# An MLA gate product with x stationary and 512 weight columns moving, and block copies from DRAM to DRAM during attention

## The chip, the cores and the metric

The kernel runs on one core of a Trainium2 chip. Its time is the time of one execution on the device, in microseconds (us); lower is better. Three runs of the kernel before gave 1257.67 to 1261.07 us, with a median of 1259.69 us. Profiles come from one further execution, recorded by the hardware profiler.

The engines are TensorE (PE; its weight loads are PEld), VectorE (DVE), ScalarE (ACT), GpSimd (POOL) and SyncE (SP). TensorE multiplies a stationary 128x128 operand by a moving operand of up to 512 columns into PSUM. SP does no arithmetic here: it issues nearly all DMAs, one after the other, and waits in its queue for what each of them needs.

## What is computed

One layer of a hybrid encoder, on x of 2048 tokens by 1024. One input projection feeds two mixers: GLA (gated linear attention, 4 heads of 128) and MLA (latent attention, 4 heads of 128). Each mixer's output is gated, both are laid side by side, projected, added to x, and normalized:

```python
h = x @ w_in
g_q, g_k, g_v, g_gate, g_lr_f, g_lr_b, m_cq, m_ckv, m_kr, m_gate = split(h)
o_a = rms_norm(o_fwd + o_bwd, norm_g) * silu(g_gate)     # GLA
o_b = softmax(scores(m_cq, m_ckv, m_kr)) @ v * silu(m_gate)   # MLA
x = layer_norm(ALPHA * x + concat([o_a, o_b]) @ w_out)
```

The change is about `silu(m_gate)`, with `m_gate = x @ w` of 2048 x 512, and about how it and `o_a` get from tokens on partitions to channels on partitions, as the last projection needs them. Every product is made in float32 with each operand split into a high and a low part (`hi` rounds, `lo` subtracts) and three matmuls: high by high, high by low, low by high (`mm3`, L417).

## The kernel before

**Stages.** Sweep A (from the start to about 345 us of the span) goes over 16 chunks of 128 tokens and makes GLA's intra-chunk part and gate. Sweep C (about 345 to 580) goes over 8 steps of two chunks. Attention (about 580 to 1110) goes over 16 blocks, each of one head and 512 queries, and over 8 pairs of key tiles in a block; towards its end the output projection begins, whose 16 chunks run until the end.

**Sweep C, one step.** For each chunk: `ipm` (L1341, the projection to cq, ckv and kr), `Ob` (L1506, GLA's inter-chunk part), then `oib`, `sqO`, `ss`, `rgl`, `rgd`, `og` (the norm and gate of GLA's output, L1509 to L1530), `oT` (a transpose in blocks of 32x32 on VectorE) and `soT` (its store to `oa_s`). From the same `ipm` come `sqm`, `ssm`, `rml`, `rmd`, `cq` (the norm of cq), then `tm` (L1413, TensorE transposes), `cqTh`, `cqTl`, `pqr` (L1437, the rotary query), `qrf` to `qrTl`, and once a step `pq` (L1296, the absorbed query) with `qah`, `qal` and `sqa` (its high and low part and their stores).

**The gate product before.** `pz` (L1257 to L1273) is made once a step, with 128 weight columns stationary and x of both chunks moving, 256 columns: 4 heads x 8 slices of the model dimension x 3 = 96 matmuls in 8 parts of 12. The result has channels on partitions already. `gm1`, `gm2`, `gm3` (ACT: exp, ln, exp on 1024 columns) and `gm4` (DVE) make the silu, `sgm` stores it to `gm_s`, whose rows here are 256 columns.

**The order of the work.** Tables written by hand set it: `PLACE_C`, with `PLACE_C_FIRST` and `PLACE_C_LAST` for the first and last step (L147 to L344). Each operation has a place in units of steps, of the step it belongs to; two values are those of the two chunks, eight those of the parts of `pz`. `sweep_c` sorts all by step plus place, and each engine, SP too, runs its own in exactly that order (`in_order`, L381). So an instruction that waits holds back all that its engine has behind it. Attention has such tables as well (`PLACE`, `PLACE_LAST`, `PLACE_OUT`), with a key-tile pair as the unit and 8 units to a block.

**Buffers.** PSUM tiles of tag "gp" (two buffers) hold `pz`, `Ob` and `pq` in turn. In SBUF, tag "gm" has one buffer, which serves the gate's `gm` and then `qal` of the same step; tag "og" has two, for `og`. A tile that takes over a buffer waits for the last user of it, which for a stored tile is the landing of its store.

**Attention's DMAs.** `fetch` (L1567), ten DMAs on SP a block, brings the queries of the block after next; `yc` (L1773) stores a block's output to `ob_s`.

**The output projection.** `OutProj.load` (L1944) issues seven DMAs on SP for a chunk: four of `oa_s` to `of`, each putting 32x32 blocks in place by rows of 32 numbers (128 bytes; `blocks_of`, L1142), one each of `gm_s` and of the softmax sums `r_s` to `gr`, and one of `ob_s` to `of`. `gate` (L1962, POOL) multiplies, `hi` (ACT) and `lo` (POOL) split, `part` and `product` (L1988, L1996) make the matmuls (`po`, `pmb`, `px`), `residual` and `finish` (L2026, L2035) add x and normalize on VectorE, and SP stores the rows.

Of the kernel before, what the change touches and what calls it, by code (L numbers as in the profile page):

```python
# [23 lines left out]
H = 4  # L24
# [108 lines left out]


SETUP_C = ("lset", "u15", "u14", "wS", "wH", "wL", "pb0", "wa0", "wh0", "wl0", "pb1", "wa1", "wh1", "wl1")
STEP_C = ("gm1", "gm2", "gm3", "gm4", "sgm", "pq", "qah", "qal", "sqa")
CHUNK_C = ("lx", "xh", "xl", "lS", "lq", "lo", "lu", "sqm", "ssm", "rml", "rmd", "cq", "ckv", "krf", "krfa",
    "krsh", "krsl", "vh", "vl", "kvx", "tm", "cqTh", "cqTl", "ckvTh", "ckvTl", "krT", "pqr", "qrf", "qrfa",
    "tq", "qrTh", "qrTl", "Sf1", "Sf2", "M", "Ob", "oib", "sqO",
    "ss", "rgl", "rgd", "og", "oT", "soT")  # L140

FETCH_C = ("lx", "xh", "xl")
LAST_C = ("ckvTh", "ckvTl", "krT")
# [51 lines left out]
    lx=(-0.578, -0.186),  # L195
    soT=(1.119, 1.45),
    pz=(0.25, 0.306, 0.318, 0.429, 0.527, 0.531, 0.557, 0.559),
    gm1=0.823,
    gm2=0.832,
    gm3=0.837,  # L200
    gm4=0.845,
    sgm=1.17,
    pq=1.435,
    qah=1.501,
# [69 lines left out]
    gm1=0.643,  # L274
    gm2=0.815,
    gm3=0.82,
    gm4=0.83,
    sgm=1.056,
    pq=1.431,
    qah=1.57,  # L280
# [8 lines left out]
    ipd=(0.042, 0.445),  # L289
    Ob=(0.0, 0.425),  # L290
    tm=(0.495, 1.083),
    pqr=(0.749, 1.284),
    tq=(0.95, 2.1),
    xh=(-0.262, -0.109),
    sqO=(0.15, 0.435),
# [18 lines left out]
    krf=(0.139, 0.6),  # L314
    cqTl=(0.598, 1.211),
    ckvTl=(0.88, 1.703),
    qrf=(0.795, 1.556),
    qrTl=(1.081, 2.186),
    xl=(-0.244, 0.3),
    M=(-0.531, -0.11),  # L320
# [2 lines left out]
    krfa=(0.255, 0.636),  # L323
    krsl=(0.395, 0.879),
    vl=(0.968, 2.242),
    qrfa=(0.871, 2.029),
    lS=(-0.721, -0.203),
    lq=(-0.357, 0.05),
    lo=(-0.14, 0.045),
# [1 line left out]
    lx=(-0.48, -0.573),  # L331
    soT=(1.29, 2.304),
    pz=(0.572, 0.578, 0.707, 0.845, 0.918, 1.023, 1.1, 1.22),
    gm1=1.309,
    gm2=1.608,
    gm3=1.859,
    gm4=1.953,
    sgm=2.042,
    pq=1.525,
    qah=1.948,  # L340
# [13 lines left out]
class K:  # L354
# [151 lines left out]
    def run(self):  # L506
        tc, nc, ins = self.tc, self.nc, self.ins
        with ExitStack() as top:
            cp = top.enter_context(tc.tile_pool(name="const", bufs=1))
            self.cp = cp  # L510
            dp = top.enter_context(tc.tile_pool(name="scr", bufs=1, space=DRAM))
            self.qd_s = [dp.tile([P, H * P], F32, name=f"qd_s{c}") for c in range(NCH)]
            self.oi_s = [dp.tile([P, H * P], F32, name=f"oi_s{c}") for c in range(NCH)]
            self.su_s = [dp.tile([P, H * P], F32, name=f"su_s{c}") for c in range(NCH)]
            self.u_s = [dp.tile([P, H * P], F32, name=f"u_s{c}") for c in range(NCH)]
            self.qa_s = [[dp.tile([P, H, QB], F32, name=f"q{p}_s{b}") for p in "hl"] for b in range(NQB)]
            self.qr_s = [dp.tile([2, QB // P, P, 256], F32, name=f"qr_s{b}") for b in range(NQB)]
# [737 lines left out]


    def c_pz(self, s, n):  # L1257
        last = s["st"] == NCH // 2 - 1
        if n == 0:
            s["pz"] = self.gp.tile([P, H, 256], F32, tag="gp", name=f"pz{s['st']}")  # L1260
        order = [(h, k) for h in range(H) for k in range(NK)]
        if last:
            order = [(h, k) for p in range(2) for k in range(NK) for h in (p, p + 2)]
        x2 = lambda t, k: t[:, k].rearrange("p a t -> p (a t)")
        part = [(h, k, p) for h, k in order[4 * n:4 * n + 4] for p in range(3)]
        if n == 0 and s["st"]:

            part.sort(key=lambda e: e[2] == 1)
        stop = {h: (k, p) for h, k, p in part if k == NK - 1}
        for h, k, p in part:  # L1270
            w, x = ((0, self.xch), (0, self.xcl), (1, self.xch))[p]
            self.nc.tensor.matmul(s["pz"][:, h], self.Wz[k][w][:, h * P:(h + 1) * P], x2(x, k),  # L1272
                                  start=(k == 0 and p == 0), stop=stop.get(h) == (k, p))  # L1273

    def c_gm1(self, s):
        s["gm"] = self.w1.tile([P, H, 256], F32, tag="gm", name=f"gm{s['st']}")
        self.nc.scalar.activation(s["gm"], s["pz"], AF.Exp, scale=-1.0)

    def c_gm2(self, s):
        self.nc.scalar.activation(s["gm"], s["gm"], AF.Ln, bias=1.0)  # L1280

    def c_gm3(self, s):
        self.nc.scalar.activation(s["gm"], s["gm"], AF.Exp, scale=-1.0)

    def c_gm4(self, s):
        self.nc.vector.tensor_tensor(s["gm"], s["pz"], s["gm"], ALU.mult)

    def of_step(self, s):
        return s["st"] // 2, slice((s["st"] % 2) * 256, (s["st"] % 2) * 256 + 256)

    def c_sgm(self, s):
        b, qs = self.of_step(s)
        self.nc.sync.dma_start(self.gm_s[b][:, :, qs], s["gm"])

    def c_pq(self, s):
        pq = s["pq"] = self.gp.tile([P, H, 256], F32, tag="gp", name=f"pq{s['st']}")  # L1296
# [8 lines left out]
        self.hi(s["qh"], s["pq"])  # L1305

    def c_qal(self, s):
        s["ql"] = self.w1.tile([P, H, 256], F32R, tag="gm", name=f"qal{s['st']}")
        self.lo(s["ql"], s["pq"], s["qh"])

    def c_sqa(self, s):
        b, qs = self.of_step(s)
        for t, dst in zip((s["qh"], s["ql"]), self.qa_s[b]):
            self.nc.sync.dma_start(dst[:, :, qs], t.bitcast(F32))

    def c_sqr(self, s, j):
        b, qs = self.of_step(s)
# [249 lines left out]
    def fetch(self, i):  # L1567
# [6 lines left out]
        for n, p in enumerate("hl"):  # L1574
            q.append(qp.tile([P, QB], F32R, tag="wz", name=f"r{p}{i}"))
            src = self.qr_s[b][n].rearrange("c (b r) (m t) -> m r (c b) t", b=4, t=32)
            for r in range(4):
                nc.sync.dma_start(q[-1][32 * r:32 * r + 32].rearrange("p (c t) -> p c t", t=32).bitcast(F32),
                                  src[2 * h + r % 2])

    def attention(self):
        tc, nc = self.tc, self.nc
        mm = nc.tensor.matmul
# [2 lines left out]
        with ExitStack() as ctx:  # L1586
# [218 lines left out]
            for i in range(nb):  # L1805
# [98 lines left out]
class OutProj:  # L1904
# [39 lines left out]
    def load(self, o):  # L1944
# [7 lines left out]
        else:  # L1952
            gr = self.gr[c % 2] = self.gr.get(c % 2) or self.slot(f"gr{c}").rearrange("p a (b d) -> p a b d", b=4)
        o["gr"] = gr
        for r, src in kern.blocks_of(kern.oa_s[c].rearrange("h p (m t) -> h p m t", t=32)):
            nc.sync.dma_start(of[r, 0].rearrange("p h (b t) -> p (h b) t", t=32), src)
        nc.sync.dma_start(gr[:, 0], kern.gm_s[b][:, :, cs])
# [161 lines left out]
```

## Time and profile before

| | |
|---|---|
| median of three runs | 1259.69 us |
| the profiled execution | 1264.79 us |
| its span, first to last instruction | 1262.9 us |
| mean granted TensorE clock | 0.997 of full speed |
| VectorE, ScalarE, GpSimd busy | 71%, 58%, 58% of the span |
| data moved by DMA | 165.59 MB in 277393 packets |

In a row of the profile, `pz<-xch,wzh` names what an instruction writes and what it reads, by the program's names; shapes are partitions x elements; L1272 is line 1272 of the kernel. What stands in brackets behind a row is how long the engine was idle before it, and what ended that idle time. Matmuls overlap: a matmul of 128x256 is shown as 0.28 us long, while the next one starts 0.12 us after it. "To landing" is from the issue of a DMA to the last byte. SPq is SP's queue: its durations are the issuing of DMAs alone.

### The profile page before, as it was taken

Reading aid. Unit: us, or ns where it says so; the run is one execution under the profiler, and the core shown is the slowest. Engines: PE = TensorE matmul, PEld = TensorE weight load, DVE = VectorE, ACT = ScalarE, POOL = GpSimd, SP = SyncE. Lnnn points to the kernel's source line nnn. Section 1 sums busy time; section 2 is a strip of 40 time slices with the busy share of each in tenths; the row PEclk is TensorE's granted clock in tenths of the full one; section 3 lists DMA queues with packets and bytes.
Section 4 is the critical chain, followed back from the end, with each engine's and each line's share of the span. In section 5 each row is a group of like instructions: output and inputs, shape, how many; then the busy total and the mean of one; then the engine's idle time right before and its main releaser. Section 6 shows DMA issues by size and latency. Waiting matters only on the chain.

```text
span 1262.9 us, 19554 instructions
## 1 busy us (share of the span) xinstructions
PE 1239.1 (98%) x6848; PEld 1089.6 (86%) x6848; DVE 896.3 (71%) x1666; ACT 729.1 (58%) x1149; POOL 726.5 (58%) x443
## 2 busy tenths in 40 slices
PE   7999999999999999999999999999999999999997
PEld 7999999999899999988788888888888888887886
DVE  6635454554565666665899999999999998378767
ACT  6643434444564444544888888888888888411210
POOL 0132323232355556530798888889999999935551
PEclk9999999999999999999999999999999999999999
DMA  8225555555757788868412222202234110487773
GB/s 294 68 84 130 134 143 139 144 139 144 266 180 212 212 247 244 245 184 210 79 28 49 43 50 43 53 15 59 59 93 93 41 42 26 125 206 212 198 210 100
DMA packets 277393, 165.59 MB, mean 131 GB/s; under 512 B 178630, under 2 KB 234830, under 8 KB 277296
## 3 DMA queue, kind: packets, MB, share of 16 engines
q1 hardware_dynamic: 276176, 162.23, 48.3%
q0 software_dynamic: 672, 2.10, 0.4%
q8 instruction: 54, 0.88, 0.3%
q14 instruction: 43, 0.35, 0.1%
q10 hardware_dynamic: 448, 0.03, 0.0%
HBM read 105.54 MB, written 58.75 MB: 130 GB/s over the span
## 4 chain that ended last, share of the span: by engine, by line
PE 84%; DVE 4%; DMA 4%; POOL 2%; issue 2%; ACT 2%; SPq 1%; DVEq 0%; POOLq 0%; ACTq 0%
PE pz L1272 7%; PE ipm L1341 5%; PE pS L1605 5%; PE pS L1607 4%; PE pS L1606 4%; PE pS L1608 4%; PE pS L1609 4%; PE o L421 4%; PE o L419 4%; PE o L420 4%; PE ipa L419 4%; PE ipa L421 4%; PE ipa L420 4%; PE ipg L421 2%; PE ipg L419 2%
## 5 line engine op out<-in xcount | busy, mean ns | idle before, releaser
L371 POOL TENSOR_TENSOR pl<-s,ph 128x1024 fp32r<-128x1024 f32 x128 | 306.8, 2416 | 47.2 <-ACT ph L365 37.0
L1614 ACT ACTIVATE s<-pS 128x1024 f32<-128x1024 f32 x128 | 131.5, 1028 | 52.9 <-PE pS L1609 49.0
L1627 DVE TENSOR_TENSOR rm<-pS,rm 128x512 f32<-128x512 f32 x210 | 144.6, 689 | 18.3 <-ACT s L1614 12.7
L1651 DVE TENSOR_TENSOR s<-s,mb 128x1024 f32<-128x1024 f32 x128 | 151.2, 1213 | 9.0 <-PE mb L1645 8.9
L365 ACT ACTIVATE ph<-s 128x1024 fp32r<-128x1024 f32 x128 | 134.8, 1056 | 15.7 <-PE o L421 15.1
L1655 ACT ACTIVATE s<-s 128x1024 f32<-128x1024 f32 x128 | 131.6, 1051 | 10.3 <-DVE s L1651 9.6
L419 PE MATMUL ipa<-wah,xah 128*128 128x384 f32 (+1 forms) x384 | 129.2, 336 | 6.1 <-ACT wah L365 6.1
L420 PE MATMUL ipa<-wal,xah 128*128 128x384 f32 (+1 forms) x384 | 125.0, 325 | 0.0
L421 PE MATMUL ipa<-wah,xal 128*128 128x384 f32 (+1 forms) x384 | 124.7, 325 | 0.0
L1091 POOL TENSOR_TENSOR Sb<-Sb,Us 64x512 f32<-64x512 f32 x15 | 19.9, 1327 | 171.5 <-DVE Us L1083 162.3
L1605 PE MATMUL pS<-qh,kvT 128*128 128x512 f32 x256 | 102.6, 401 | 0.8 <-DVE rm L1627 0.4
L419 PE MATMUL o<-ph,vh 128*128 128x512 f32 x256 | 100.9, 394 | 0.0
L1607 PE MATMUL pS<-qh,kvT 128*128 128x512 f32 x256 | 100.0, 391 | 0.0
L1606 PE MATMUL pS<-ql,kvT 128*128 128x512 f32 x256 | 100.0, 390 | 0.0
L421 PE MATMUL o<-ph,vl 128*128 128x512 f32 x256 | 99.8, 390 | 0.0
L1608 PE MATMUL pS<-rh,kvT 128*128 128x512 f32 x256 | 99.8, 390 | 0.0
L1609 PE MATMUL pS<-rl,kvT 128*128 128x512 f32 x256 | 99.8, 390 | 0.0
L420 PE MATMUL o<-pl,vh 128*128 128x512 f32 x256 | 99.7, 389 | 0.0
L1678 DVE TENSOR_TENSOR ap<-ap,s 128x512 f32<-128x512 f32 x120 | 82.9, 691 | 2.7 <-ACT s L1655 0.7
L419 PEld LDWEIGHTS ipa<-wah,xah 128*128 128x128 f32 x384 | 73.3, 191 | 9.3 <-ACT wah L365 6.4
L371 POOL TENSOR_TENSOR ol<-of,oh 128x512 fp32r<-128x512 f32 x32 | 42.5, 1328 | 59.8 <-ACT oh L365 47.4
L1272 PE MATMUL pz<-xch,wzh 128*128 128x256 f32 x256 | 73.4, 290 | 1.4 <-DVE og L1529 1.3
(308 smaller groups left out, 3404.9 us busy)
## 6 DMA issues: line engine op xcount, KB each, us to landing
xcf<-xT_dram SPq DMA_DIRECT2D x16, 512.0 KB, 5.5
xr<-x_dram SPq DMA_DIRECT2D x16, 512.0 KB, 6.0
out_dram<-rr SPq DMA_DIRECT2D x32, 256.0 KB, 3.5
xaf<-xT_dram SPq DMA_DIRECT2D x14, 512.0 KB, 4.2
oib<-oi_s SPq DMA_DIRECT2D x16, 256.0 KB, 4.9
qdb<-qd_s SPq DMA_DIRECT2D x16, 256.0 KB, 3.5
SU<-su_s SPq DMA_DIRECT2D x16, 256.0 KB, 5.0
ub<-u_s SPq DMA_DIRECT2D x16, 256.0 KB, 4.1
```

Of the source, the lines that this page charges most:

```text
L371: return e.tensor_tensor(dst, src, hi.bitcast(F32), ALU.subtract).ins
L419: mm(out, ah, bh, start=start, stop=False)
L420: mm(out, ah, bl, start=False, stop=False)
L421: mm(out, al, bh, start=False, stop=stop)
L1272: self.nc.tensor.matmul(s["pz"][:, h], self.Wz[k][w][:, h * P:(h + 1) * P], x2(x, k), start=(k == 0 and p == 0), stop=stop.get(h) == (k, p))
L1605: mm(ps[:, e], kh, qh, start=True, stop=False)
L1606: mm(ps[:, e], kh, ql, start=False, stop=False)
L1607: mm(ps[:, e], kl, qh, start=False, stop=False)
L1608: mm(ps[:, e], kr, rh, start=False, stop=False)
L1609: mm(ps[:, e], kr, rl, start=False, stop=True)
L1627: V.tensor_tensor(d["rm"], src[:, e], d["rm"], ALU.max)
L1651: V.tensor_tensor(s, s, d["mb"][:, None, :].to_broadcast([P, 2, QB]), ALU.subtract)
```

## The change

**The product.** `pz` now holds tokens on partitions, 512 channels for each of the two chunks: x of one chunk is stationary, 512 columns of the weight move. A step has 2 chunks x 8 slices x 3 = 48 matmuls, in 8 parts of 6; the first four parts make the first chunk's half, the last four the second's.

**The gate.** `gm1` to `gm4` run once per chunk, on 512 columns each; `gm4` writes back into PSUM, and a new `gmx` transposes it in 32x32 blocks into SBUF. The store goes to `gm_s`, now with one tensor a step, as blocks.

**`qal`** leaves the "gm" buffer for two tiles of 256 x 2 columns in "og", so that `sqa` has three stores where it had two.

**The copies.** `place_blocks`, new, is put once for each chunk into attention's order, behind a block's `fetch` (4.05 and 6.05 in a block): eight DMAs on SP from DRAM to DRAM, four that put the blocks of `oa_s` and four that put those of `gm_s` in place in a new `og_s`, in rows of 128 bytes at both ends. `OutProj.load` then has one DMA each for the two halves of `og_s`, four DMAs in all.

**Places.** `gm1` to `gm4` and `gmx` get two places each; in the last step `pqr`, `qrf` and `qrfa` of the first chunk move back.

```diff
-STEP_C = ("gm1", "gm2", "gm3", "gm4", "sgm", "pq", "qah", "qal", "sqa")
+STEP_C = ("sgm", "pq", "qah", "qal", "sqa")
...
-    gm1=0.823,
-    gm2=0.832,
-    gm3=0.837,
-    gm4=0.845,
+    gm1=(0.45, 0.823),
+    gm2=(0.46, 0.826),
+    gm3=(0.47, 0.829),
+    gm4=(0.745, 0.832),
+    gmx=(0.76, 0.835),
...
-    pqr=(0.749, 1.284),
+    pqr=(0.88, 1.284),
...
-    qrf=(0.795, 1.556),
+    qrf=(0.885, 1.556),
...
-    qrfa=(0.871, 2.029),
+    qrfa=(0.89, 2.029),
...
-    gm1=1.309,
-    gm2=1.608,
-    gm3=1.859,
-    gm4=1.953,
+    gm1=(0.8785, 1.309),
+    gm2=(0.91, 1.608),
+    gm3=(1.2, 1.859),
+    gm4=(1.26, 1.953),
+    gmx=(1.265, 1.954),
...
-            self.gm_s = [dp.tile([P, H, QB], F32, name=f"gm_s{b}") for b in range(NQB)]
+            self.gm_s = [dp.tile([2, H, P, P], F32, name=f"gm_s{s}") for s in range(NCH // 2)]
...
+            self.og_s = [dp.tile([P, 2, H, P], F32, name=f"og_s{c}") for c in range(NCH)]
...
     def c_pz(self, s, n):
...
-            s["pz"] = self.gp.tile([P, H, 256], F32, tag="gp", name=f"pz{s['st']}")
...
-        for h, k, p in part:
-            w, x = ((0, self.xch), (0, self.xcl), (1, self.xch))[p]
-            self.nc.tensor.matmul(s["pz"][:, h], self.Wz[k][w][:, h * P:(h + 1) * P], x2(x, k),
-                                  start=(k == 0 and p == 0), stop=stop.get(h) == (k, p))
+            s["pz"] = self.gp.tile([P, 2, 512], F32, tag="gp", name=f"pz{s['st']}")
+        j, half = divmod(n, 4)
+        for k in (2 * half, 2 * half + 1):
+            xh, xl = self.xch[:, k, j], self.xcl[:, k, j]
+            self.mm3(s["pz"][:, j], xh, xl, self.Wz[k][0], self.Wz[k][1], start=(k == 0), stop=(k == NK - 1))
...
+    def c_gm4(self, d):
+        gm, pz = self.gm(d)
+        self.nc.vector.tensor_tensor(pz, pz, gm, ALU.mult)
+
+    def c_gmx(self, d):
+
+        self.nc.vector.transpose(*self.gm(d))
...
-        s["ql"] = self.w1.tile([P, H, 256], F32R, tag="gm", name=f"qal{s['st']}")
-        self.lo(s["ql"], s["pq"], s["qh"])
+        s["ql"] = []
+        for n in range(2):
+            hs = slice(2 * n, 2 * n + 2)
+            s["ql"].append(self.w1.tile([P, 2, 256], F32R, tag="og", name=f"qal{s['st']}_{n}", bufs=2))
+            self.lo(s["ql"][n], s["pq"][:, hs], s["qh"][:, hs])
...
+    def place_blocks(self, c):
+
+        for n, scr in enumerate((self.oa_s[c], self.gm_s[c // 2][c % 2])):
+            for r, src in self.blocks_of(scr.rearrange("h p (m t) -> h p m t", t=32)):
+                self.nc.sync.dma_start(self.og_s[c][r, n].rearrange("p h (b t) -> p (h b) t", t=32), src)
...
+            for c in range(NCH):
+                put(NP * min(c, nb - 2) + 6.05, self.place_blocks, c)
...
-        for r, src in kern.blocks_of(kern.oa_s[c].rearrange("h p (m t) -> h p m t", t=32)):
-            nc.sync.dma_start(of[r, 0].rearrange("p h (b t) -> p (h b) t", t=32), src)
-        nc.sync.dma_start(gr[:, 0], kern.gm_s[b][:, :, cs])
+        nc.sync.dma_start(of[:, 0], kern.og_s[c][:, 0])
+        nc.sync.dma_start(gr[:, 0], kern.og_s[c][:, 1])
```

More of the change, by code (lines that the diff above doesn't have):

```diff
@@ L139 @@
     "tq", "qrTh", "qrTl", "Sf1", "Sf2", "M", "Ob", "oib", "sqO",
-    "ss", "rgl", "rgd", "og", "oT", "soT")
+    "ss", "rgl", "rgd", "og", "oT", "soT", "gm1", "gm2", "gm3", "gm4", "gmx")
 FETCH_C = ("lx", "xh", "xl")
@@ L273 @@
     pz=(-0.249, -0.195, -0.111, -0.018, 0.405, 0.452, 0.485, 0.622),
[L274 to L277, printed above, removed]
+    gm1=(0.623, 0.643),
+    gm2=(0.6231, 0.815),
+    gm3=(0.6232, 0.82),
+    gm4=(0.65, 0.83),
+    gmx=(0.81, 0.835),
     sgm=1.056,
@@ L1257, in c_pz @@
     def c_pz(self, s, n):
-        last = s["st"] == NCH // 2 - 1
         if n == 0:
-            s["pz"] = self.gp.tile([P, H, 256], F32, tag="gp", name=f"pz{s['st']}")
[L1261 to L1268, printed above, removed]
@@ L1269, in c_pz @@
-        stop = {h: (k, p) for h, k, p in part if k == NK - 1}
-        for h, k, p in part:
-            w, x = ((0, self.xch), (0, self.xcl), (1, self.xch))[p]
-            self.nc.tensor.matmul(s["pz"][:, h], self.Wz[k][w][:, h * P:(h + 1) * P], x2(x, k),
-                                  start=(k == 0 and p == 0), stop=stop.get(h) == (k, p))
-    def c_gm1(self, s):
-        s["gm"] = self.w1.tile([P, H, 256], F32, tag="gm", name=f"gm{s['st']}")
-        self.nc.scalar.activation(s["gm"], s["pz"], AF.Exp, scale=-1.0)
@@ L1279, in c_gm2 @@
[L1279 to L1286, printed above, removed]
+            s["pz"] = self.gp.tile([P, 2, 512], F32, tag="gp", name=f"pz{s['st']}")
[3 more added lines that the diff above has]
+            self.mm3(s["pz"][:, j], xh, xl, self.Wz[k][0], self.Wz[k][1], start=(k == 0), stop=(k == NK - 1))
@@ new lines, in gm, with c_gm1, c_gm2, c_gm3 @@
+    def gm(self, d):
+        s, j = d["step"], d["j"]
+        if "gm" not in s:
+            s["gm"] = self.w1.tile([P, 2, 512], F32, tag="gm", name=f"gm{s['st']}")
+        return s["gm"][:, j], s["pz"][:, j]
+    def c_gm1(self, d):
+        gm, pz = self.gm(d)
+        self.nc.scalar.activation(gm, pz, AF.Exp, scale=-1.0)
+    def c_gm2(self, d):
+        gm, _ = self.gm(d)
+        self.nc.scalar.activation(gm, gm, AF.Ln, bias=1.0)
+    def c_gm3(self, d):
+        gm, _ = self.gm(d)
+        self.nc.scalar.activation(gm, gm, AF.Exp, scale=-1.0)
@@ L1288, in of_step @@
+    def c_gm4(self, d):
+        gm, pz = self.gm(d)
+        self.nc.vector.tensor_tensor(pz, pz, gm, ALU.mult)
+    def c_gmx(self, d):
+        self.nc.vector.transpose(*self.gm(d))
     def of_step(self, s):
@@ L1291, in c_sgm @@
     def c_sgm(self, s):
-        b, qs = self.of_step(s)
-        self.nc.sync.dma_start(self.gm_s[b][:, :, qs], s["gm"])
+        self.nc.sync.dma_start(self.gm_s[s["st"]].rearrange("j h p f -> p (j h) f"),
+                               s["gm"].rearrange("p j (h f) -> p (j h) f", h=H))
     def c_pq(self, s):
@@ L1307, in c_qal @@
     def c_qal(self, s):
-        s["ql"] = self.w1.tile([P, H, 256], F32R, tag="gm", name=f"qal{s['st']}")
-        self.lo(s["ql"], s["pq"], s["qh"])
+        s["ql"] = []
[3 more added lines that the diff above has]
+            self.lo(s["ql"][n], s["pq"][:, hs], s["qh"][:, hs])
     def c_sqa(self, s):
         b, qs = self.of_step(s)
-        for t, dst in zip((s["qh"], s["ql"]), self.qa_s[b]):
-            self.nc.sync.dma_start(dst[:, :, qs], t.bitcast(F32))
+        qh, ql = self.qa_s[b]
+        self.nc.sync.dma_start(qh[:, :, qs], s["qh"].bitcast(F32))
+        for n, t in enumerate(s["ql"]):
+            self.nc.sync.dma_start(ql[:, 2 * n:2 * n + 2, qs], t.bitcast(F32))
     def c_sqr(self, s, j):
```

## The prediction

> **What bounds the kernel now.** I read the page first (busy time, chain), then busy time by stage, then who waited for whom on TensorE, then timelines around each wait.
>
> ```profile
> span 1262.9 us, 19554 instructions
> PE 1239.1 (98%) x6848; PEld 1089.6 (86%) x6848; DVE 896.3 (71%) x1666; ACT 729.1 (58%) x1149; POOL 726.5 (58%) x443
> ...
> PE 84%; DVE 4%; DMA 4%; POOL 2%; issue 2%; ACT 2%; SPq 1%; DVEq 0%; POOLq 0%; ACTq 0%
> ```
>
> TensorE is busy 98% of the span and makes 84% of the chain that ended last. By stage (window, length, PE busy, PEld, DVE, ACT, POOL, clock, DMA share, GB/s), a middle step of sweep C and then most of attention:
>
> ```profile
> 440.00:468.00 28.00, 28.00 (x206) 27.30 (x205) 17.78 (x63) 14.20 (x38) 15.50 (x17) 1.00 0.82 238
> 612.00:1078.00 466.00, 466.00 (x2118) 383.53 (x2117) 422.24 (x572) 394.67 (x423) 424.55 (x184) 1.00 0.23 49
> ```
>
> Both stages are TensorE's alone: not a gap, at full clock. So a time is saved only where TensorE gets less to do or where it stands still, and its waits are few (total us, times, longest):
>
> ```profile
> PE pz L1272 <- DVE og L1529: 1.3, 2, 0.9
> PE pqr L421 <- DVE cqT_l L371: 1.3, 1, 1.3
> PE ipm L1341 <- POOL xcl L371: 1.0, 1, 1.0
> PE pmb L421 <- POOL ol L371: 1.0, 1, 1.0
> PE rt L1747 <- ACT rt L1753: 0.8, 1, 0.8
> PE tm L1413 <- ACT cq L1364: 0.8, 1, 0.8
> ...
> PE pmb L419 <- ACT oh L365: 0.3, 1, 0.3
> ...
> PE pq L419 <- DVE og L1529: 0.3, 1, 0.3
> ```
>
> The rows with pz, pqr, ipm, tm and pq lie in sweep C, those with pmb and rt in the output projection.
>
> **Term 1, the product: -4.9.** The mean duration of a matmul misleads, because matmuls overlap; what counts is the distance from start to start. The chain gives it for the 256-column form (start, us, what); for the new form, x stationary and 512 weight columns moving, sweep A's gate product already has it:
>
> ```profile
> 440.53 4.31 PE pz L1272 x36
> ...
> 468.19 0.83 PE pz L1272 x7
> ```
>
> ```profile
> 345.18 0.39 PE L421 MATMUL ipg<-wgh,xbl 128*128 128x512 f32 x1
> ...
> 348.58 0.39 PE L421 MATMUL ipg<-wgh,xbl 128*128 128x512 f32 x1
> ```
>
> 4.31/36 = 0.1197 us each; 15 starts from 345.18 to 348.58 are 0.2267 us each. Columns are streamed as often as before (8 steps x 96 x 256 = 8 steps x 48 x 512), so only what is paid once per matmul is halved: 768 x 0.1197 = 91.9 becomes 384 x 0.2267 = 87.0. As TensorE has no gap here, all 4.9 count, 0.6 in each step of 27.66 us (468.19 - 440.53). If the new form cost twice the old one, the term would be nothing; I take the measured form.
>
> The Trainium skill, "TensorE: Matmul & The Clock Gate", section "Back-to-back issue gap", has a lone matmul's gap as N/2.4 + 2.5 ns: estimated 109 and 216 ns, which would leave a gain of only 1.0 us. Neither distance agrees with the rows.
>
> **Term 2, the gate's arithmetic: nothing.** Three activations and a product on 1024 columns become two sets on 512, with two transposes added.
>
> ```profile
> 456.77 1.02 ACT L1277 ACTIVATE gm<-pz 128x1024 f32<-128x1024 f32 x1
> ```
>
> ```profile
> 352.00 0.63 ACT L1559 ACTIVATE ub<-ub 128x512 f32<-128x512 f32 x1
> ```
>
> ```profile
> L1509 DVE TENSOR_TENSOR Ob<-Ob,oib 128x512 f32<-128x512 f32 x11 | 7.6, 694 | 0.7 <-PE Ob L1506 0.7
> L1535 DVE STREAM_TRANSPOSE oT<-og 128x512 f32<-128x512 f32 x10 | 7.1, 712 | 0.3
> ...
> L1286 DVE TENSOR_TENSOR gm<-pz,gm 128x1024 f32<-128x1024 f32 x5 | 6.1, 1225 | 31.7 <-ACT gm L1283 31.7
> ```
>
> ACT: 6 x 0.63 for 3 x 1.02, 0.7 more in a step. DVE: 2 x 0.69 + 2 x 0.71 for 1.22, and qal cut in two (1.22 into 2 x 0.69) 0.2 more: 1.8 in a step. Both have over 10 us idle in a step by the window row; the first half's activations fall under pq's matmuls, the second set ends before the old one did, because the xh split (0.81) no longer waits for the last pz part. Its cover gone, 2 us in 8 steps would be 16.
>
> **Term 3, waits in steps 1 and 2: -2.2.** Here one buffer was the cause. qal of step 0 sat in gm's buffer, and gm1 of step 1 had to wait for its store to land:
>
> ```profile
> 400.31 1.03 ACT L1277 ACTIVATE gm<-pz 128x1024 f32<-128x1024 f32 x1 [2.46 <-DMA qr_s<-qrT]
> ```
>
> (The row names the store issued next on that queue; the buffer is qal's.)
>
> ```profile
> 403.55 1.22 DVE L1286 TENSOR_TENSOR gm<-pz,gm 128x1024 f32<-128x1024 f32 x1 [8.78 <-ACT gm L1283]
> ...
> 409.93 1.13 DVE L1529 SCALAR_TENSOR_TENSOR og<-Ob,rg_r,ub 128x128 f32<-128x128 f32 x4
> ```
>
> Behind gm4 VectorE runs nearly without a gap to og, for which pz of step 2 waits, and tm waits for cq behind the same work. With qal in "og" buffers that wait is gone, gm of the second half ends some 4 us sooner, and the queue starts at its inputs. The rows pz<-og, tm<-cq and pq<-og make 2.4; I take 2.2, bounds 0 and 2.4.
>
> **Term 4, new tightness: +0.9.** In the last step pqr of the first chunk moves from 0.749 to 0.88, behind pz's fourth part:
>
> ```profile
> 569.58 0.42 DVE L1546 TENSOR_TENSOR qrf<-pqr,cos 128x256 f32<-128x256 f32 x1 [1.45 <-PE pqr L421]
> ```
>
> ```profile
> 572.43 0.47 ACT L1364 ACTIVATE cq<-ipm,rm_r 128x256 f32<-128x256 f32 x1 [3.50 <-DVE rm_r L446]
> ```
>
> ```profile
> 573.69 0.38 PE L1413 MATMUL tm<-ident,cq 128*128 128x128 f32 x2
> ```
>
> Ahead of pqr stand 24 matmuls of 0.2267 (5.4) where there were 36 of 0.1197 (4.3), so qrf starts 1.0 later (5.4 against the 4.4 at which pqr went out), and queued behind it on VectorE are qrx and rm_r, for which cq waits, for which tm waits. From cq's end (572.90) to tm there were 0.8; TensorE comes to tm 0.5 sooner and cq 1.0 later: 0.7 lost, the value I take (0 to 0.9). In the middle steps pq needs og's buffer:
>
> ```profile
> 445.07 1.13 DVE L1529 SCALAR_TENSOR_TENSOR og<-Ob,rg_r,ub 128x128 f32<-128x128 f32 x4
> ```
>
> og ends at 446.20, pq started at 446.81 and will want to start 0.5 sooner: 0.1 left, so 0.2 over all steps (0 to 0.6). The waits pqr<-cqT_l and ipm<-xcl follow Ob through VectorE with no gate work between; they stay.
>
> **Term 5, the copies and the loads: 0 and -2.0.** 128 DRAM copies of 64 KB go to SP during attention, after each block's fetch. SP there is idle for long:
>
> ```profile
> 693.04 2.33 SPq L1578 DMA_DIRECT2D rl<-qr_s  x4
> 719.24 0.34 SPq L1777 DMA_DIRECT2D ob_s<-yc  x1
> ```
>
> ```profile
> L1956 SPq DMA_DIRECT2D of<-oa_s x64: 303/482/1547, 935.4 to 1219.8; - x64
> ...
> DMA to landing us min/median/max: 1.9/4.0/8.4
> ```
>
> A copy from DRAM to DRAM is not in this trace. Nearest are the old loads in the same 128-byte pieces, above: 0.48 us of SP each, 4.0 to landing. Its bounds are nothing, where SP is idle, and the last rival below. Eight copies are 4 us of the 24 in which SP waited from 695.4 to 719.2, so nothing; the fetch behind them keeps its lead of over a block (128 matmuls of 512 columns, 29.0 us).
>
> In the projection a chunk's load falls from seven DMAs to four. This is the chain behind the waits of pmb:
>
> ```profile
> 1107.08 1.92 SPq L1956 DMA_DIRECT2D of<-oa_s  x4
> 1109.09 1.44 SPq L1957 DMA_DIRECT2D gr<-gm_s  x1
> ...
> 1128.30 2.73 SPq L2048 DMA_DIRECT2D out_dram<-rr  x4
> ```
>
> ```profile
> 1135.35 1.29 DVE L2032 SCALAR_TENSOR_TENSOR rr<-xr,po 128x512 f32<-128x512 f32 x2 [1.78 <-DMA out_dram<-rr]
> ```
>
> ```profile
> 1165.21 0.69 DVE L2032 SCALAR_TENSOR_TENSOR rr<-xr,pmb 128x512 f32<-128x512 f32 x1 [5.49 <-DMA xr<-x_dram]
> ```
>
> The first output stores stand on SP behind the loads of three chunks; VectorE waits for them, behind it ACT's oh and POOL's ol, and for these pmb; rt waits behind an x load that SP issued late. Three loads shortened by 1.4 us each (four DMAs in 1.92, against about 0.5 for one) move that by more than the 1.0 and 0.8 waited. The three rows make 2.1; I take 2.0, bounds 0 and 2.1. From 1170 on TensorE has no wait, so more cannot come.
>
> **Sum.** -4.9 - 2.2 + 0.9 - 2.0 = -8.2. The profiled execution took 1264.79 us (span 1262.9), 5.1 above the median 1259.69; its own time becomes 1256.6, and the median 1251.5, 0.65% less. A measurement of this kernel tells about 0.3% (3.8 us) from no change.
>
> **Rivals.**
> *Only the product counts:* the waits stay or move one place, since nearly every one is followed on its engine by another queue. 1259.7 - 4.9 = 1254.8. For it: pqr and ipm wait in the last step for the same VectorE. Against it: the causes of terms 3 and 5 are taken away, not covered.
> *The product gains nothing:* the change doesn't do what it says, a pair of 256 costs what one of 512 does, 2 x 0.1197 = 0.2394 instead of 0.2267. The other terms give 1256.4. Against it stand the 15 distances of 0.2267 with just these shapes. By the Trainium skill's gap rule (page and section above) 1.0 of the 4.9 would be left, 1255.4.
> *A new wait takes the place of the old:* gm has one buffer, and gm1 of the next step's first half now comes 0.37 of a step sooner, when the store of gm must have landed.
>
> ```profile
> 466.63 0.53 SPq L1293 DMA_DIRECT2D gm_s<-gm  x1
> ```
>
> ```profile
> 446.81 0.28 PE L419 MATMUL pq<-cqT_h,wabs_h 128*128 128x256 f32 x1
> ```
>
> gm1 is wanted when pq starts, at 446.81 + 27.66 - 0.5 = 474.0, 7.3 after the issue; about 1 more is hidden under pq, then qah, cq and tm are late. It decides from a landing of 8.3 us. Rows of 256 columns become rows of 128 here, and the longest landing above is 8.4. At 9.3 each of 7 steps loses 1 us: 1258.4.
> *The copies hold up SP (the other side):* in each block SP must issue ten fetches (about 6 us by the row of four), a store (0.3) and eight copies. If writing 128-byte pieces to DRAM held SP up at each issue, it would decide from (29.0 - 6.3)/8 = 2.8 us a copy; from there the fetches fall back block by block, and TensorE waits for q. At 3.1, twice the longest issue above (1.55), 2.1 us are lost in each of 14 blocks: 29 less 8.2, 1280.5. For it: pieces of 128 bytes at both ends, 65536 in all. Against it: a DMA share of 0.23 in attention.
> The Trainium skill, "DMA: Bandwidth & Descriptors", section "Specifications", says that below 512 bytes the DMA reads, modifies and writes; no run here shows what that costs between two places in DRAM.
>
> **How the numbers follow.** Forecast 0.60 (1248 to 1254.5); only the product 0.14; product nothing 0.05; new wait 0.08; copies on SP 0.06; better than forecast, the waits of pqr and ipm gone too (2.3 more, 1249 and below), 0.07. The likeliest gives 1251.5. The range runs from 1247.5 (-4.9 - 2.4 - 2.1 - 2.3 = -11.7, and a little) to 1257.5, which leaves out the copies and most of the new wait, 0.14. Faster by over 0.3%: the forecast, the better case, three quarters of the product alone and a part of the third: 0.79. Within: the rest of these two and most of the new wait, 0.14. Slower: the copies and the rest of it, 0.07.
>
> **What would show it.** Term 1: 24 pz matmuls in 5.4 us, 0.6 less in each step, whose length becomes 27.0 to 27.1. Term 3: no wait of gm1 of step 1 for a DMA, no rows pz<-og and tm<-cq. Term 4: a wait of tm for cq in the last step. Term 5: no waits of pmb and rt, and SP past its copies before the next yc. I am wrong if a step is longer than 27.4, if ACT shows gm waiting for gm_s, if attention lasts longer than its 466 us for the same window, or if the projection keeps its 2.1 us of waits.

## The result, and the profile after

The kernel after took 1256.74 us (median of 12 runs, 1255.75 to 1258.12), the kernel before 1259.81 us in the 12 runs beside them (1257.67 to 1261.96). The ratio is 0.9974, 95% interval 0.9965 to 0.9983: 3.07 us less, where 8.2 less were forecast. Runs in which the granted clock of the whole execution was low are left out of every comparison below.

The profiled execution of after took 1256.90 us. Its page (span, TensorE's busy time, shares of the chain):

```profile
span 1255.1 us, 18903 instructions
...
PE 1234.6 (98%) x6464; PEld 1069.0 (85%) x6464; DVE 910.0 (73%) x1698; ACT 732.4 (58%) x1173; POOL 728.2 (58%) x443
...
PE 93%; DVE 2%; issue 2%; ACT 1%; DMA 1%; POOL 1%; SPq 0%; DVEq 0%; POOLq 0%; ACTq 0%
```

From profile to profile the span fell by 7.8 us (1262.9 to 1255.1), nearly the forecast sum; from median to median, by 3.07. The two differ because the profiled execution of before lay 5 us above its own median and that of after lies on it. So there are two questions: what was in those 5 us, and what did the change do to an ordinary execution?

TensorE's waits in the kernel after (us in all, times, longest), the counterpart of the table in the prediction:

```profile
PE ipa L422 <- ACT wah L368: 5.2, 2, 4.9
PE pz L422 <- DVE og L1541: 1.8, 2, 1.1
PE pqr L424 <- DVE cqT_l L374: 1.3, 1, 1.3
PE ipm L1353 <- POOL xcl L374: 1.0, 1, 1.0
...
PE pq L422 <- DVE og L1541: 0.4, 1, 0.4
PE tm L1425 <- ACT cq L1376: 0.4, 1, 0.4
```

pmb and rt wait no longer. But pz waits for og longer than before (1.8 against 1.3), and the longer of its two waits lies at another place.

The stages can be told apart by the first matmul of a tile: ipm begins sweep C, pq ends a step, pS begins attention, po the projection. The distances in us, for four profiled executions ("before again" is the first experiment; "mended" is the last version below):

| stage | before, profiled | before again | after | mended |
|---|---|---|---|---|
| start to the first ipm | 348.81 | 347.15 | 348.22 | 347.54 |
| to pq of step 0 | 38.92 | 38.92 | 39.85 | 38.22 |
| to pq of step 1 | 31.42 | 29.03 | 27.27 | 27.27 |
| steps 2 to 5 | 110.64 | 110.64 | 108.67 | 108.75 |
| step 6 | 29.30 | 29.32 | 29.04 | 29.05 |
| step 7 | 18.61 | 18.59 | 19.48 | 18.44 |
| last pq to pS | 2.80 | 2.81 | 2.81 | 2.80 |
| attention, pS to po | 479.49 | 479.46 | 479.70 | 479.68 |
| po to the last matmul's end | 195.11 | 194.48 | 192.24 | 192.23 |

Between the two ordinary executions, columns 2 and 3, the sum is -3.1: the start +1.07, which has nothing to do with the change (over all profiles of this study, of both kernels and their variants, the first ipm came between 346.9 and 348.8), step 0 +0.93, step 1 -1.76, steps 2 to 5 -1.97, step 6 -0.28, step 7 +0.89, attention +0.24, projection -2.24.

### The profile page after: what moved, and what is told of

The parts are those of the page before. It is cut to its first block, busy times and chain, and to the rows that moved or that the text cites. A ratio compares the mean times of both kernels' runs of the same rounds, so it can differ in the third digit from the quotient of the medians.

```text
span 1255.1 us, 18903 instructions
## 1 busy us (share of the span) xinstructions
PE 1234.6 (98%) x6464; PEld 1069.0 (85%) x6464; DVE 910.0 (73%) x1698; ACT 732.4 (58%) x1173; POOL 728.2 (58%) x443
## 4 chain that ended last, share of the span: by engine, by line
PE 93%; DVE 2%; issue 2%; ACT 1%; DMA 1%; POOL 1%; SPq 0%; DVEq 0%; POOLq 0%; ACTq 0%
PE ipm L1353 5%; PE ipa L422 5%; PE o L422 5%; PE o L424 5%; PE o L423 5%; PE ipa L423 5%; PE ipa L424 5%; PE pS L1623 5%; PE pS L1625 5%; PE pS L1624 5%; PE pS L1627 4%; PE pS L1626 4%; PE po L423 3%; PE po L424 3%; PE po L422 3%; PE ipg L424 2%
## 5 line engine op out<-in xcount | busy, mean ns | idle before, releaser
L423 PEld LDWEIGHTS ipa<-wal,xah 128*128 128x128 f32 x384 | 73.7, 192 | 1.0 <-DVE wal L374 0.5
L424 PEld LDWEIGHTS ipa<-wah,xal 128*128 128x128 f32 x384 | 73.7, 192 | 0.1
```

The costliest lines, as they stand in the source:

```text
L423: mm(out, ah, bl, start=False, stop=False)
L424: mm(out, al, bh, start=False, stop=stop)
```

## The experiments

**The kernel before, again, twice.** No edit.

> The kernel before, unchanged, in another execution. Theory A (the profiled execution of before, 1264.8 us, was 5 us above its median because part of the waits that terms 3 and 5 of the prediction count happened in that execution and not in most): the span comes out near 1257.8 us, and TensorE's waits pz for og, tm for cq, pq for og, pmb for ol and oh and rt for rt sum to under 2 us instead of 4.5. Theory B (the waits are there in every execution, and what the change saved on them was taken back by new waits in the kernel after): the same rows come again with about 4.5 us, whatever the span.

Its span was 1258.2 us (time 1260.07). The waits came again: pz for og 1.3, pq for og 0.3, pmb for ol 1.0, rt 0.6; only tm for cq and pmb for oh were gone. They make 3.2 us, between the two theories: the span came out as theory A has it, but most of these waits are usual. The difference to the profiled execution lies in step 1, 29.03 us against 31.42, and there in two things. First gm1's wait for qal's store, which was 2.46 us in the row of the prediction:

```profile
397.75 1.03 ACT L1277 ACTIVATE gm<-pz 128x1024 f32<-128x1024 f32 x1 [1.58 <-DMA ql_s<-qal]
```

With the store 0.9 us earlier tm does not wait, and only one pause of TensorE is left. Second, the granted clock. Windows of the profiled execution of before (busy time of PE, PEld, DVE, ACT and POOL with their counts, then the granted clock, DMA share and GB/s):

```profile
408.00:412.00 4.00, 2.29 (x18) 1.87 (x17) 3.24 (x14) 2.47 (x13) 3.61 (x3) 1.00 0.97 293
412.00:416.00 4.00, 4.00 (x23) 4.00 (x23) 3.88 (x17) 2.15 (x8) 3.07 (x4) 0.57 0.72 192
```

Behind the two pauses TensorE is fully busy, but at 0.57 of its clock for 4 us: 23 matmuls, where the same stretch of the ordinary execution has 36 at full clock:

```profile
410.00:414.00 4.00, 4.00 (x36) 4.00 (x35) 3.83 (x16) 1.76 (x8) 3.38 (x5) 1.00 0.63 192
```

No wait table shows this, since nothing waits. Was it a single event?

> The kernel before, unchanged, once more. If the dip of the granted clock in step 1 (4 us at 0.61 and 0.54 in the profiled execution) belongs to that execution alone: no dip, step 1 of 28.5 to 29.1 us, gm1 of step 1 waiting 1 to 1.6 us for the store, and 1.3 to 2.1 us of waits of pmb and rt. If it is usual: the dip again, step 1 near 31.4 us, a span near 1262 us.

It was not. This execution took 1263.45 us (span 1261.6), with the long wait again and the dip again:

```profile
398.56 1.03 ACT L1277 ACTIVATE gm<-pz 128x1024 f32<-128x1024 f32 x1 [2.47 <-DMA qr_s<-qrT]
```

```profile
410.00:414.00 4.00, 4.00 (x23) 4.00 (x23) 3.93 (x17) 2.02 (x8) 2.92 (x5) 0.59 0.72 187
```

Step 1 lasted 31.40 us. In four profiles with the old buffers there are thus two kinds of execution: qal's store lands early (gm1 waits 1.2 to 1.6 us, step 1 of 28.6 to 29.0 us) or late (2.5 us, 31.4). The profile shown was of the late kind, and the median lies near the early one: the early execution of before took 1260.07 us, the two late ones 1264.79 and 1263.45, and the medians of before are 1259.81 beside the result and 1260.45 to 1261.09 in the three sets of this study. How many of the executions without a profile were of either kind is not known.

**Term 3 alone: qal in og's buffers, in the kernel before.**

```diff
-        s["ql"] = self.w1.tile([P, H, 256], F32R, tag="gm", name=f"qal{s['st']}")
-        self.lo(s["ql"], s["pq"], s["qh"])
...
+            s["ql"].append(self.w1.tile([P, 2, 256], F32R, tag="og", name=f"qal{s['st']}_{n}", bufs=2))
+            self.lo(s["ql"][n], s["pq"][:, hs], s["qh"][:, hs])
...
```

> The kernel before with qal in two tiles of og's buffers instead of one of gm's, and three stores for two; nothing else. Term 3 as predicted: 2.2 us less than the kernel before, with no wait of gm1 of step 1 for a store. By the other execution of the kernel before, where gm1 waited 1.58 us and step 1 lasted 29.03 us against 27.66 for the next: 1.2 to 1.4 us less. If the wait only moves to another engine: the same time as before.

Measured: 1259.04 us (1258.11 to 1260.86) against 1260.45 (1258.53 to 1263.10), 0.9991 (0.9982 to 1.0000), 1.4 us less; the interval just reaches no change, so the size rests on the trace. gm1 of step 1 starts without a wait, and step 1 lasts 27.70 us:

```profile
396.44 1.01 ACT L1277 ACTIVATE gm<-pz 128x1024 f32<-128x1024 f32 x1
```

The mechanism of term 3 is shown; in an ordinary execution it is worth 1.3 (29.03 less 27.70), not 2.2. Two of the waits that the term counted are still there, the first in the last step, the second in step 0:

```profile
PE pz L1272 <- DVE og L1534: 0.4, 1, 0.4
PE pq L419 <- DVE og L1534: 0.3, 1, 0.3
```

**Term 1 alone: after, with the product in halves of 256 columns.** x stays stationary.

```diff
+        g, lower = divmod(half, 2)
+        w = slice(256 * g, 256 * g + 256)
+        for k in range(4 * lower, 4 * lower + 4):
...
+            self.mm3(s["pz"][:, j, w], xh, xl, self.Wz[k][0][:, w], self.Wz[k][1][:, w],
...
```

> The kernel after with the gate product cut in halves of 256 weight columns, x stationary as before the cut: 768 matmuls instead of 384. Term 1 as predicted: 4.9 us more than the kernel after, 1261.6 us; by the length of its middle steps (27.16 us against 27.66) 4.0 us more. If the product gained nothing: the same time as after. By the gap rule of the Trainium skill 1.0 us more.

Measured: 1260.38 us (ten runs, 1260.00 to 1261.21), 0.9995 of the kernel before (0.9986 to 1.0004), 3.6 above after's 1256.76. The product gains, so the rival does not hold. Nor does the 1.0 by the gap rule of the Trainium skill ("TensorE: Matmul & The Clock Gate", section "Back-to-back issue gap"). Steps 2 to 5 are back at 27.66 each, so a step gains 0.49. Steps 0 and 1, 40.36 and 27.71, are 0.51 and 0.47 longer than in after's second profile. Steps 6 and 7 together are 49.02 here and 48.52 to 49.01 in five profiles of after and of variants with the same last step, four of them 48.82 or more: there, halving the matmuls gains 0.5 at most, and mostly 0.2. And a part of the 3.6 is not the product: attention took 480.53 us here, against 479.70 and 479.90 in after, with a wait at its start that no other profile has:

```profile
PE pS L1630 <- DMA rl<-qr_s: 0.9, 1, 0.9
```

By the stages of sweep C the product is worth 2.9 to 3.4 in all.

**Term 5 alone: the copies of the GLA output, in the kernel before.**

```diff
...
+            for c in range(NCH):
+                put(NP * min(c, nb - 2) + 6.05, self.place_blocks, c)
...
-            nc.sync.dma_start(of[r, 0].rearrange("p h (b t) -> p (h b) t", t=32), src)
+        nc.sync.dma_start(of[:, 0], kern.og_s[c])
```

> The kernel before with the copies of the GLA output alone, loaded in the projection by one DMA; product and gate as before. Theory B (term 5 holds): 2.0 us less than before, 1257.8 us. Theory A: within 0.7 us of the kernel before.

Measured: 1259.80 us against 1261.09, 0.9990 (0.9982 to 0.9999), 1.3 us less, between the two theories. From the first to the last instruction it is 2.0 less, as forecast (medians of the spans 1257.3 and 1259.3): the time of a run is 2.5 us longer than its span here and 1.8 in the other kernels, and what that 0.7 is the traces do not show. In its profile pmb and rt do not wait. What the waits cost differs from one execution of before to the next: the starts of TensorE in the projection were late by 2.6 us (profiled), 1.9, 3.1, and 1.3 where only qal was moved.

**After without the copies.** The projection loads blocks of both arrays itself.

```diff
...
-        nc.sync.dma_start(of[:, 0], kern.og_s[c][:, 0])
-        nc.sync.dma_start(gr[:, 0], kern.og_s[c][:, 1])
+        for t, scr in ((of, kern.oa_s[c]), (gr, kern.gm_s[c // 2][c % 2])):
+            for r, src in kern.blocks_of(scr.rearrange("h p (m t) -> h p m t", t=32)):
+                nc.sync.dma_start(t[r, 0].rearrange("p h (b t) -> p (h b) t", t=32), src)
```

> The kernel after without its copies: the projection loads the blocks of both arrays itself, ten DMAs a chunk. Theory B (term 5 holds): the waits of pmb and rt, 2.1 us, come back, and as the loads are longer than before the change, some more: 1258.8 us or above, against 1256.7. Theory A (most executions have no such waits): within 1 us of 1256.7, unless ten DMAs a chunk are late themselves.

Measured: 1265.54 us, 1.0043 (1.0029 to 1.0057), 8.8 above after. That is above what theory B asked for, but it does not decide between the two, since ten DMAs a chunk are late themselves. A chunk's blocks hold SP for 5 us and more, and TensorE starts late at nine places of the projection:

```profile
1118.40 2.91 SPq L1969 DMA_DIRECT2D of<-oa_s  x4
1121.35 2.56 SPq L1969 DMA_DIRECT2D gr<-gm_s  x4
```

```profile
PE pmb L422 <- DVE rr L2044: 2.8, 4, 1.2
...
PE pmb L424 <- POOL ol L374: 1.7, 2, 1.0
...
PE rt L1759 <- ACT rt L1765: 1.1, 1, 1.1
PE pmb L422 <- ACT oh L368: 1.0, 1, 1.0
```

With the gate's output stored by tokens, the kernel without the copies would be slower than before; they are what makes the new layout pay. They themselves cost nothing that the trace shows. SP takes some 5.3 us for eight of them, where 4 were forecast, and is past them before each next yc. In after (duration of an issue in ns, least/median/longest, and the landing):

```profile
L1597 SPq DMA_DIRECT2D og_s<-oa_s x64: 528/627/1368, 597.6 to 1000.3; - x64
L1597 SPq DMA_DIRECT2D og_s<-gm_s x64: 528/627/1440, 600.2 to 1003.2; - x64
...
DMA to landing us min/median/max: 2.2/2.6/3.9
```

**After, again, as a yardstick.**

> The kernel after, unchanged, as the yardstick of the other runs of this set. By the stages of one more execution of the kernel before (span 1258.2 us, no dip of the granted clock) the change is worth 3 to 4.5 us between typical executions: 0.9965 to 0.9975 of the kernel before. If instead the prediction's sum of 8.2 us held between typical executions, 0.9935.

1256.76 us against 1260.45, 0.9967 (0.9955 to 0.9980): 3.7 us less. (All kernels compared with after, above and below, are compared with this median, also where they ran in another set; the ratios are to the kernel before of their own set, whose median was 1260.45 to 1261.09 us.) Step 0 and step 1 were 39.85 and 27.24 us, as in the first profile.

**Step 0 mended.** Here the kernel after loses. The first step's table, which the diff of the change above does not show, was changed with the rest; `og` of the first chunk has the place 0.804 in both kernels:

```diff
-    gm1=0.643,
-    gm2=0.815,
-    gm3=0.82,
-    gm4=0.83,
+    gm1=(0.623, 0.643),
+    gm2=(0.6231, 0.815),
+    gm3=(0.6232, 0.82),
+    gm4=(0.65, 0.83),
+    gmx=(0.81, 0.835),
```

VectorE's and TensorE's rows in step 0 of the kernel after:

```profile
366.94 0.16 DVE L449 TENSOR_TENSOR rg_r<-rg_t,Ob 128x4 f32<-128x4 f32 x1
370.82 0.70 DVE L1289 TENSOR_TENSOR pz<-pz,gm 128x512 f32<-128x512 f32 x1 [3.72 <-ACT gm L1277]
371.43 1.12 DVE L1541 SCALAR_TENSOR_TENSOR og<-Ob,rg_r,ub 128x128 f32<-128x128 f32 x4
...
379.91 1.13 DVE L1541 SCALAR_TENSOR_TENSOR og<-Ob,rg_r,ub 128x128 f32<-128x128 f32 x4
```

```profile
381.09 0.50 PE L422 MATMUL pz<-wzh,xch 128*128 128x512 f32 x1 [1.12 <-DVE og L1541]
```

At 367.1 og has all it needs, but gm4 of the first half stands ahead of it (places 0.65 and 0.804) and waits 3.7 us for the three activations. From there VectorE runs with one gap, of 0.48 us, to og of the second chunk, for which pz of step 1 waits.

```diff
-    pz=(-0.249, -0.195, -0.111, -0.018, 0.405, 0.452, 0.485, 0.622),
-    gm1=(0.623, 0.643),
-    gm2=(0.6231, 0.815),
-    gm3=(0.6232, 0.82),
-    gm4=(0.65, 0.83),
+    pz=(-0.249, -0.195, -0.111, -0.018, 0.4145, 0.452, 0.485, 0.622),
+    gm1=(0.4142, 0.643),
+    gm2=(0.4151, 0.815),
+    gm3=(0.4152, 0.82),
+    gm4=(0.8052, 0.83),
```

> The kernel after with step 0 mended: the first chunk's three activations ahead of pz's second half, its product behind og and oT on VectorE. Theory C (the 1.28 us at which pz of step 1 waits for og, and a part of the 0.54 us of pq for og, come from VectorE standing 3.7 us at gm4 of chunk 0 with og queued behind it, so that term 2's price of nothing was wrong here): 1.3 to 1.9 us less than the kernel after. Rival (og of chunk 1 is late for what it needs itself, Ob and the norm, and the gate's order is beside the point): within 0.4 us of the kernel after.

1254.54 us, 0.9951 (0.9938 to 0.9965), 2.2 less than after. In its rows og comes first. From the start of sweep C (347.19 us here, 348.22 in after) og of the second chunk comes 1.6 us sooner, and pz does not wait for it; pq's wait for og, 0.4 us, stays:

```profile
366.10 1.13 DVE L1541 SCALAR_TENSOR_TENSOR og<-Ob,rg_r,ub 128x128 f32<-128x128 f32 x4
...
367.97 0.70 DVE L1289 TENSOR_TENSOR pz<-pz,gm 128x512 f32<-128x512 f32 x1
...
377.26 1.13 DVE L1541 SCALAR_TENSOR_TENSOR og<-Ob,rg_r,ub 128x128 f32<-128x128 f32 x4
```

Step 0 fell from 39.85 to 38.23 us, 1.6 less; the medians say 2.2.

**Only gm4 moved.**

```diff
-    gm4=(0.65, 0.83),
+    gm4=(0.8052, 0.83),
```

> The kernel after with only the product gm4 of step 0's first half moved on VectorE, behind og and oT; its three activations stay where they are, at the end of pz. If the order on VectorE's queue is what costs the 1.28 us: 1.2 to 1.6 us less than the kernel after, about 1255.3 us. If the late activations cost it: within 0.4 us of the kernel after, while the version that moved them too took 2.2 us less.

1255.66 us, 0.9951 (0.9939 to 0.9964), 1.1 less than after; step 0 was 38.79 us. Neither case as expected: by the trace the order on VectorE's queue is two thirds of it (1.06 of 1.62 us), by the medians half. The rest goes with the late activations: behind og and oT, VectorE still stands 1.81 us at gm4 of the first half, which it does not where they were moved too. The ratios to the kernel before of each set are the same for both versions, so the split rests on one trace of each.

**The last step, pqr back at its old place.**

```diff
-    pqr=(0.88, 1.284),
+    pqr=(0.749, 1.284),
...
-    qrf=(0.885, 1.556),
+    qrf=(0.795, 1.556),
...
-    qrfa=(0.89, 2.029),
+    qrfa=(0.871, 2.029),
```

> The kernel after with pqr, qrf and qrfa of the last step's first chunk back at their old places, ahead of pz's fourth part. Term 4 (this move costs 0.7 us, by 0.51 and 0.29 us of tm waiting for cq in the profile after): 0.7 to 0.9 us less than the kernel after. Rival (cq would be late all the same because sweep C's last step has less product to hide it under): within 0.3 us of the kernel after.

1257.06 us, 0.9971 (0.9960 to 0.9983), 0.3 above after: nothing gained. The wait of tm for cq is gone, and this has come in its place:

```profile
565.74 0.60 ACT L1277 ACTIVATE gm<-pz 128x512 f32<-128x512 f32 x1 [1.78 <-PE pz L424]
```

```profile
566.39 0.50 PE L422 MATMUL pz<-wzh,xch 128*128 128x512 f32 x1 [0.69 <-ACT gm L1277]
```

pz's second half is written to the tile whose first half gm1 reads, and its first matmul waits for that read. In the kernel after, pqr stands between the two and covers it. The time is the rival's, the reason is not: cq is in time, and there was a second wait, which the move of pqr avoids.

**In addition, the gate's first half behind all of pz.**

```diff
-    gm1=(0.8785, 1.309),
-    gm2=(0.91, 1.608),
-    gm3=(1.2, 1.859),
-    gm4=(1.26, 1.953),
-    gmx=(1.265, 1.954),
+    gm1=(1.2201, 1.309),
+    gm2=(1.2202, 1.608),
+    gm3=(1.2203, 1.859),
+    gm4=(1.95, 1.953),
+    gmx=(1.951, 1.954),
```

> The kernel after with pqr of the last step's first chunk at its old place again, as in the run before, and in addition all of the gate's work on the last step's first half behind the end of pz, so that pz's second half does not wait for gm1. Theory D (in the last step either pqr stands late and tm waits 0.76 us for cq, or pqr stands early and pz waits 0.85 us for gm1, since gm1 reads the tile that pz goes on writing): both waits go, 0.7 to 0.9 us less than the kernel after, 1256.0 us. Rival (TensorE waits for VectorE in this step whatever the order): within 0.3 us of it.

1255.11 us, 0.9947 (0.9934 to 0.9960), 1.65 less than after, where 0.7 to 0.9 were expected. Both waits are gone, step 7 lasts 18.72 us against 19.48 and 19.83 in after's two profiles: 0.8 to 1.1 by the trace. Of the waits in this stretch of its profile these stay:

```profile
PE pqr L424 <- DVE cqT_l L374: 1.3, 1, 1.3
PE ipm L1353 <- POOL xcl L374: 1.0, 1, 1.0
PE pz L422 <- DVE og L1541: 0.9, 1, 0.9
```

**Both mended.**

> Both mended places together: step 0 as in the version that took 1254.54 us, the last step as in the first kernel of this set. If they add up: 2.9 to 3.1 us less than the kernel after, 1253.7 us, 0.9945 of the kernel before. If the last step's gain is lost again at the start of attention: as step 0 alone, 1254.5 us.

1253.59 us, 0.9939 (0.9924 to 0.9954), 3.2 less than after, where 2.9 to 3.1 were expected. By the trace the two add up: step 0 is 1.6 shorter than in after, step 7 1.0 to 1.4. This version beats both kernels.

## Why the prediction was wrong

**The step that failed** is the sum, "its own time becomes 1256.6, and the median 1251.5", together with the size of four of its terms, above all term 2, the gate's arithmetic, which was put at nothing and cost 1.4 us in step 0.

The sum carried the 5.1 us between the profiled execution and the median over, as if they were scatter that both kernels have. Mostly they were not. Of the 4.7 us by which it lay above the ordinary execution, 2.4 lie in step 1 (31.42 against 29.03): the late landing of qal's store, tm's wait that follows from it, and the dip of the clock behind the two pauses. The change removes that store from gm's way, so the kernel after cannot have them, and its profile lies on its median. 0.63 lie in the projection. Only the start (1.66) is scatter of both kernels.

So the first half of the sentence came out, 1256.90 for 1256.6, and that was luck. From profile to profile terms 1, 2 and 4 were 3.1 worse than forecast, and step 1 in its late kind (3.7 for 2.2), the projection with attention (2.7 for 2.0) and an earlier start (0.6) gave 2.7 back. Against the ordinary execution of before the change saves 4.2 by the stages, without the start, instead of 8.2. Term by term:

1. **The product, -4.9: -3.9.** The mechanism is shown, the size was too large. Steps 2 to 5 lost 0.49 each instead of 0.6, and 3.9 is eight times that; what steps 6 and 7 take back of it is counted under 4. In place of 0.2267 us the mean distance of the new matmuls is 0.229, 11 starts from the first to the last of these rows of after:

```profile
445.31 0.39 PE L422 MATMUL pz<-wzh,xch 128*128 128x512 f32 x1
...
447.83 0.39 PE L424 MATMUL pz<-wzh,xcl 128*128 128x512 f32 x1
```

   Most distances are 0.227, as predicted, but some are 0.231 to 0.236. The 15 that the prediction took lie below the rest of sweep A: over all of that sweep's gate product the median is 0.229 to 0.230.

2. **The gate's arithmetic, 0: +1.4** (step 0's +0.93 and the 0.49 that its product should have gained; in the version with halves of 256 columns, which lacks that gain, step 0 is 1.43 longer than before). In the middle steps the price of nothing was right: the window of 28 us shows TensorE without a gap. In step 0 it was wrong, because the argument went by VectorE's idle time in a step. That time was there. What counted was the place of one gm4 in VectorE's queue, ahead of an og that was ready. Moving it and its activations gave 2.2 us back by the medians, 1.6 by the trace.

3. **Waits in steps 1 and 2, -2.2: -1.3.** The cause and the cure are shown by qal's move alone. The size was wrong in three ways. It was read from an execution of the late kind. Of the 2.4 us of waits that it counted, 0.4 (pz for og) lie in the last step and 0.3 (pq for og) in step 0, and qal's move leaves both. And the dip of the clock, 1.5 us, stands in no table of waits. In the late kind the change saves 3.7 in step 1 (31.42 less 27.27, less the product's 0.49), in the early kind 1.3.

4. **New tightness, +0.9: +1.6** (steps 6 and 7 together +0.61, and 0.98 that the product should have gained there). In after's second profile it is +2.1, as steps 6 and 7 vary by 0.5 from one profile to the next. The wait of tm for cq came as predicted: two late starts of 0.51 and 0.29 us from start to start, the second of them for ckv, which ACT makes behind cq. In addition these two steps hang on VectorE's og and cqT_l and on GpSimd's xcl, so most of the product's gain came back as waits; that the halved matmuls buy little there, 0 to 0.5 of the 0.98, is shown by the version with halves, which of the three takes how much is not. That pqr was moved at all looked like a cost only; it covered a wait of pz for gm1 that the prediction did not see.

5. **Copies 0, loads -2.0: attention +0.24, projection -2.24.** Right. The same profile has attention's middle window at 466 us of TensorE without a gap, at a DMA share of 0.34 instead of 0.23:

```profile
440.00:468.00 28.00, 28.00 (x159) 25.18 (x158) 19.63 (x72) 14.71 (x41) 15.29 (x17) 1.00 0.83 240
612.00:1078.00 466.00, 466.00 (x2117) 383.22 (x2117) 421.38 (x571) 393.91 (x421) 424.29 (x185) 1.00 0.34 68
```

   The 0.24 lies within what attention differs by between kernels without a copy: 479.33 in the second repetition of before, 479.55 in after without copies, 479.76 where only qal was moved. The loads of the GLA output alone gave 1.3 by the medians of the times, 2.0 by those of the spans.

The five come to -4.2 (-3.94 + 1.42 - 1.27 + 1.59 + 0.24 - 2.24); with after's second profile in place of the first they come to -3.5. The medians gave 3.07 and 3.7. That the start's +1.07 would make -3.1 of the -4.2 is chance. Of the rivals, the new wait of gm1 for gm_s did not appear, nor did SP fall behind. "The product gains nothing" was closest in time, 1256.4, and for the wrong reason: the product does gain, two more terms counted besides, and two losses that were priced too low took 3.0 back.

## What to carry to other kernels

When the profiled execution lies above the median by as much as the effect that is forecast, find out first which rows hold that excess (a granted clock by windows of a few us, the landing that a wait hangs on); if the change removes them, the median gains less than the profile does. When an operation is cut and its pieces are given new places, check each queue at each step, the first and the last too, for a piece that is not ready standing ahead of one that is; idle time in the step says nothing on that. And a gain in an engine's work counts only in the steps where that engine is the last to arrive.

## What the runs showed of the hardware

- **The clock can dip behind short pauses.** In two executions of before, TensorE stood still twice for about 1.0 us within 2.5 us, and behind that the granted clock was 0.50 for 3.4 us (0.57 and 0.59 as means of 4 us), which cost 1.5 us by the distances of the matmuls there:

```profile
412.44:415.85 3.41, 3.41 (x19) 3.41 (x18) 3.31 (x13) 1.83 (x8) 2.92 (x4) 0.50 0.71 174
```

  With one pause (ordinary execution of before, 0.88 us of idle time; after, 1.12 us) it stayed at 1.00. Neither pauses nor the busy share alone settle it: in after without copies TensorE came late by 1.21 and 1.18 us within 3.0 us and was busy for 1.95 us of 4, less than the 2.29 and 2.28 ahead of the two dips, and the clock stayed at 1.00. The Trainium skill, "TensorE: Matmul & The Clock Gate", section "Part 1: The HAM clock gate", puts such a dip down to a window of about 3.4 us that runs freely and to half the clock after an idle one. The length and the half agree with the row above; but TensorE was not idle in the 3.4 us ahead of the dips, it was busy for about half of them (1.77 and 1.72 us). What sets it off stays open.
- **A copy from DRAM to DRAM in pieces of 128 bytes**, 64 KB each, held SP for 0.63 us and landed after 2.6 us (2.2 to 3.9). The loads of such pieces to SBUF in the kernel before held SP for 0.48 us and landed after 4.0 us (1.9 to 8.4), beside other traffic.
